# Summing MLP weight blocks in DRAM: fewer sums, and half of them moved into the MLP

## Chip, cores, metric

The kernel runs on one core of a Trainium2 chip. The metric is the device time of one execution in microseconds (us), as a median of runs.

## What is computed

One decoder layer over 2048 tokens of width 1024, in float32, followed by a final RMSNorm. Four token mixers share one input projection; the MLP has a squared ReLU between two weights of 1024x4096 and 4096x1024.

```python
h = rms_norm(x, norm1_g); z = h @ w_in
y = concat([sgu(z), s5(z), rglru(z), forgetting_attention(z)])
x = x + group_rms_norm(y, mix_norm_g) @ w_out
h = rms_norm(x, norm2_g)
x = x + square(relu(h @ w_mlp_in)) @ w_mlp_out
out = rms_norm(x, final_g)
```

## The kernel before

Every product is made of three matmuls on high and low parts (`wh`, `wl`, and the like), so each operand is read, cast on ScalarE (the high part) and subtracted on VectorE (the low part): the helper `split`, L53 to L58.

**Order of the stages.** Input projection with the small mixers and S5 (until about 600 us), attention with the output projection woven between its units, then the MLP. Up to the MLP the order on TensorE is written by hand, with a planner clock `ck` that counts planned TensorE time; other engines are ordered by the framework. Inside `MLP.run` the framework orders all engines, in its own plan of when data is ready, earlier-traced instructions first.

**The MLP.** Tokens are processed in two halves of 1024, and the hidden width in two chunks `c` of 2048. Each (half, chunk) has an "in" stage and an "out" stage. A stage is a 2x2 block product done by Strassen's scheme with 7 products `i` instead of 8: `FIRST` and `SECOND` say for each product which two blocks of the weight and of the other operand are added or subtracted, and to which results it goes. `IN_ORDER` and `OUT_ORDER` are the orders of the products. Each product has 8 steps `p` of 12 matmuls, so a stage has 56 steps and the MLP 448 (`steps`, index `n`). For the first half, steps 0 to 55 are the in stage of chunk 0, 56 to 111 its out stage, 112 to 167 the in stage of chunk 1.

**Weights of a step.** `make(n + 2)` requests the weight of a step two steps ahead. A weight that is one block is loaded with one DMA into the pool `rw` (5 buffers, 2 KB per partition) by `weight`. A weight that is a sum of two blocks is loaded with two DMAs into one tile of the pool `raw` (`m_raw`, 5 buffers, 4 KB per partition) by `weight_pair`, and added on GpSimd (`united`, L1492). `tokens_side` loads the other operand of the next product, 4 tiles for each product, through the same pool `raw`, added on GpSimd where it is a sum. The preparation of the second token half (`prep`) runs beside the first half's in stage, one piece at every second step from step 11 on: it holds four tiles `h` of the pool `raw` from their load until the last of eight groups of four transposes (`tp`), first for tokens 0 to 511 of the half, then for the others.

**Sums in DRAM.** To save the second load and the GpSimd addition, `weight_sums` builds some sums in DRAM tables: a copy of one block from the ScalarE queue (L1426, 512 KB, DRAM to DRAM) and, three jobs later, an accumulating DMA of the other block from the GpSimd queue (L1430). `S1` are four tables of the first weight for chunk 0 (products 2, 5, 6 and 7), `S2` eight tables of the second weight, four for each chunk. Each table takes 4 jobs: 16 for `S1`, 32 for `S2`. The planner clock calls one job every 9.0 planned us from 110 on; what is left when attention ends is issued there at once (L1794).

**Around the change.** In attention the queries and keys (`q`, `ks`) are loaded from a DRAM scratch `qk`, whose high parts `qh` are stored from the ScalarE queue and low parts `ql` from the GpSimd queue. `ngc` are cumulative gates, spread over the partitions. The output projection stores its result `x1` from the GpSimd queue (L1369, shown as x<-x), and SyncE loads it again (L1348, and as `h` for the MLP).

Of the kernel before, what the change touches and what calls it, by code (L numbers as in the profile page):

```python
# [5 lines left out]
F32 = mybir.dt.float32  # L6
# [36 lines left out]
def behind(tc, eng):  # L43

    ins = next(i for i in reversed(tc.nc.cur_bb.bb.instructions) if i.engine == eng)
    return tc.issue_after(ins)
# [1349 lines left out]
IN_ORDER = (1, 4, 5, 7, 3, 2, 6)  # L1396
# [1 line left out]
AHEAD = 2  # L1398


def weight_sums(tc, w1, w2, S1, S2):

    nc = tc.nc
    jobs = []
    for c in range(2):
        def second(x):
            return w2[(c * 2 + x[0]) * 1024:(c * 2 + x[0] + 1) * 1024, x[1] * 512:(x[1] + 1) * 512]

        def first(x):
            return w1[x[1] * 512:(x[1] + 1) * 512, (c * 2 + x[0]) * 1024:(c * 2 + x[0] + 1) * 1024]

        for S, side, table, n, at in ((S1, 0, FIRST, 128, first), (S2, 1, SECOND, 256, second)):
            for i in IN_ORDER:
                if (i, c) in S:
                    a, b, _ = table[i][side]
                    for r in range(4):
                        rs = slice(r * n, (r + 1) * n)
                        jobs.append((S[i, c][rs], at(a)[rs], at(b)[rs]))  # L1420
    LAG = 3
    for n in range(len(jobs) + LAG):
        if n < len(jobs):
            to, a, _ = jobs[n]
            with behind(tc, ACT):
                nc.scalar.dma_start(out=to, in_=a)  # L1426
        if n >= LAG:
            to, _, b = jobs[n - LAG]
            with behind(tc, POOL):
                nc.gpsimd.dma_start(out=to, in_=b, accum_op=ADD)  # L1430
        yield


class MLP:
# [1 line left out]

    def __init__(self, tc, cst, final_g, x1, hT, w1, w2, S1, S2, out, T=2048):
        self.tc, self.nc, self.cst, self.x1, self.hT, self.w1, self.w2, self.out, self.T = tc, tc.nc, cst, x1, hT, w1, w2, out, T  # L1440
        self.final_g, self.S1, self.S2 = final_g, S1, S2
        self.D, self.FF = w1.shape
        self.KD = self.D // 128
        self.HT = 1024
        self.NC = 2
        self.NP = self.FF // 128 // self.NC // 2
        self.es = ExitStack()
        self.P = lambda n, b, **k: self.es.enter_context(tc.tile_pool(name=n, bufs=b, reuse_waits="tile", **k))
        P = self.P
        self.bp = P("m_b", 2)  # L1450
        self.raw = P("m_raw", 5)
        self.rw = P("m_rw", 5)
        self.wp = P("m_w", 4)
        self.htp = P("m_ht", 2)
        self.sm = P("m_sm", 2)
        self.jkp = P("m_jk", 1)
        self.ps_i = P("m_psi", 3, space=PSUM)
        self.halves = list(reversed(range(T // self.HT)))
# [71 lines left out]
    def first_weight(self, c, i, p):  # L1530

        a, b, sign = FIRST[i][0]
        rows = lambda w, f: w[:, f:f + 128].rearrange("(k p) f -> p k f", p=128)
        if (i, c) in self.S1:
            return self.weight(rows(self.S1[i, c], p * 128))
        w = [rows(self.w1[x[1] * 512:(x[1] + 1) * 512], self.tile_row(c, p, x[0])) for x in (a, b) if x]
        return self.weight_pair(w, sign) if b else self.weight(w[0])

# [67 lines left out]
    def run(self):  # L1606
        nc, P, NP = self.nc, self.P, self.NP

        P("m_pad", 1).tile([128, 32], F32, tag="pad", name="pad")
        self.cp = P("m_c", 1)  # L1610
        self.sp = P("m_s", 3)
        self.shp = P("m_sh", 4)
        accp = P("m_acc", 1)
        gp = P("m_gf", 1)
        ps_o = P("m_pso", 5, space=PSUM)
        self.C, self.acc = {}, {}
        ends = {}
        for order, table, n in ((IN_ORDER, FIRST, 0), (OUT_ORDER, SECOND, 1)):
            seen, last = {}, {}
            for i in order:  # L1620
                for blk, _ in table[i][2]:
                    seen.setdefault(blk, i)
                    last[blk] = i
            ends[n] = {i: [b for b in seen if seen[b] == i] for i in order}, {i: [b for b in last if last[b] == i] for i in order}
        steps = [(half, c, out, i, p) for half in self.halves for c in range(self.NC) for out in range(2)
                 for i in (OUT_ORDER if out else IN_ORDER) for p in range(NP)]
        made, sides = {}, {}
        groups = [s[:4] for s in steps if s[4] == 0 and not s[2]]

        def side(n):  # L1630
            if n < len(groups):
                half, _, _, i = groups[n]
                g = self.tokens_side(half, i)
                sides[groups[n]] = next(g)
                return g
            return iter(())

        def make(n):
            if n >= len(steps):
                return  # L1640
            half, c, out, i, p = steps[n]
            if not out:
                made[n] = (self.first_weight(c, i, p),)
            else:
                made[n] = self.second_weight(c, i, p), self.hidden_side(i, p)

        gf = gp.tile([128, self.D], F32, tag="gf", name="gf")
        nc.sync.dma_start(out=gf, in_=self.final_g.partition_broadcast(128))
        for _ in side(0):
            pass  # L1650
        for n in range(AHEAD):
            make(n)
        nxt, more, part = 1, iter(()), iter(())
        for n, (half, c, out, i, p) in enumerate(steps):
            if c == 0 and not out and i == IN_ORDER[0] and p == 0:
                k = self.halves.index(half) + 1
                more = self.prep(self.halves[k]) if k < len(self.halves) else iter(())
            if c == 0 and not out and i == IN_ORDER[3]:
                self.acc[p] = accp.tile([128, self.D], F32, tag=f"acc{p}", name="acc")
                with behind(self.tc, SP):  # L1660
                    nc.sync.dma_start(out=self.acc[p], in_=self.x1[half * self.HT // 128 + p])
            if n % 2 and n > 10:
                next(more, None)
            make(n + AHEAD)
            if not out and p == 1:
                part = side(nxt)
                nxt += 1
            if not out and 1 <= p < 6:
                next(part, None)
            got = made.pop(n)  # L1670
            first, last = (e[i] for e in ends[out])
            if not out:
                self.product_in(i, p, got[0], sides[half, c, out, i], first, last)
                continue
            if p == 0:
                po = [ps_o.tile([128, 512], F32, tag="po", name="po") for _ in range(4)]
            self.product_out(p, *got, po)
            if p == NP - 1:
                for t in range(4):
                    for (rt, d), sign in SECOND[i][2]:  # L1680
                        self.gather(self.acc[4 * rt + t][:, d * 512:(d + 1) * 512], po[t], sign)
                    if c == self.NC - 1:
                        for rt in range(2):

                            if (rt, 0) in last and all((rt, 1) not in e for e in later(ends[1][1], i)) or \
                                    (rt, 1) in last and all((rt, 0) not in e for e in later(ends[1][1], i)):
                                self.finish(half, 4 * rt + t, gf)
        self.es.close()
# [10 lines left out]


RATES = 2.3, 0.5
SUMS = 110.0, 9.0
NX, NO, XB = 2, 3, 2


def hybrid_kernel(tc, A, out, T=2048):
    nc = tc.nc
    with ExitStack() as top:
# [9 lines left out]
                 v=dp.tile([T, 4, 2, 64], F32, name="v"), ys=dp.tile([T, 1024], F32, name="ys"),  # L1718
                 negc=dp.tile([4, T], F32, name="negc"), x1=[dp.tile([128, 1024], F32, name=f"x1_{t}") for t in range(T // 128)],
                 hT=[[dp.tile([128, 512], F32, name=f"hT_{k}_{q}") for q in range(T // 512)] for k in range(8)])  # L1720
        S1 = {(i, 0): dp.tile([512, 1024], F32, name=f"s1_{i}0") for i in IN_ORDER if FIRST[i][0][1] and i != 1}
        S2 = {(i, c): dp.tile([1024, 512], F32, name=f"s2_{i}{c}") for i in OUT_ORDER if SECOND[i][1][1] and i != 1 for c in range(2)}
        D5 = s5_scratch(dp)
        r8 = cp.tile([128, NPR], F32, name="r8")
# [11 lines left out]
            cst["ii"] = ii  # L1736

        ck = Clock()
        sums = weight_sums(tc, A["w_mlp_in"][0], A["w_mlp_out"][0], S1, S2)
        ck.set_slow(sums, *SUMS)  # L1740
        with tc.manual_schedule(engines={mybir.EngineType.PE}):
            side = ExitStack()
# [50 lines left out]
            ea.close()  # L1793
            for _ in sums:  # L1794
                pass
            M = MLP(tc, cst, A["final_g"], S["x1"], S["hT"], A["w_mlp_in"][0], A["w_mlp_out"][0], S1, S2, out, T)
            ps_t[0] = pool(eo, "o_pst", 2, space=PSUM, side="right")
            at.idle = False
            ps_o[0] = [(pool(eo, "o_pso2", NO, space=PSUM, side="right"), "po")]
# [40 lines left out]
```

## Time and profile before

| what | us |
| --- | --- |
| median of 3 runs | 2517.39 |
| lowest and highest of them | 2511.12, 2519.61 |
| profiled execution, its own time | 2509.57 |
| its span in the trace | 2507.9 |
| TensorE busy in the span | 2201.3 (88%) |

The span runs from the first to the last instruction of one profiled execution. Rows of stages give each engine's busy time in a stretch, the clock that TensorE was granted (1.00 is 2.4 GHz), the mean busy share of the 16 DMA engines and the rate that they moved. The in and out stages of the MLP were cut where the matmuls change from `pi` (in) to `po` (out).

### The profile page before, as it was taken

To read this page: it belongs to the slowest core of one execution; us is meant where nothing else is said; L and a number is where in the kernel's file an instruction comes from. 1 tells how busy PE (TensorE), PEld (TensorE's weight loads), DVE (VectorE), ACT (ScalarE), POOL (GpSimd) and SP (SyncE) were. 2 spreads that over 40 slices of the span, in tenths; PEclk is the share of its full clock that TensorE was granted. 3 is DMA by queue.
4 is the path that set the end of the run, shared out by engine and by line. 5 is a ranking of instruction groups with operands and counts; after the bars stand their busy time and mean duration, and the time that the engine had idled before them with its cause. 6 is when DMAs were issued, how large, how long until landed. Compare 5 with 4: busy or idle time off the path is not lost.

```text
span 2507.9 us, 32062 instructions
## 1 busy us (share of the span) xinstructions
PE 2201.3 (88%) x10077; PEld 1792.2 (71%) x10077; DVE 1672.5 (67%) x3776; ACT 1169.5 (47%) x2351; POOL 832.4 (33%) x908
## 2 busy tenths in 40 slices
PE   5798987894779978677899999999999999999997
PEld 5676766673567767565777778878778887888886
DVE  6686755662446655343668786787986769668697
ACT  4312534252345545332567434575355753457543
POOL 2143343232001101020312472554722237245462
PEclk8899998997789989798999999999999999999999
DMA  7535457546577776478876544874448533487323
GB/s 177 143 66 132 122 144 203 156 117 184 163 183 204 224 215 185 131 251 284 258 253 190 168 129 132 236 234 136 134 150 281 183 124 126 127 232 230 126 89 110
DMA packets 367963, 434.52 MB, mean 173 GB/s; under 512 B 42352, under 2 KB 244112, under 8 KB 367536
## 3 DMA queue, kind: packets, MB, share of 16 engines
q1 hardware_dynamic: 319696, 327.46, 42.9%
q0 software_dynamic: 32704, 73.54, 11.9%
q10 hardware_dynamic: 15392, 31.46, 4.0%
q8 instruction: 80, 1.31, 0.2%
q14 instruction: 91, 0.75, 0.1%
HBM read 369.30 MB, written 113.34 MB: 192 GB/s over the span
## 4 chain that ended last, share of the span: by engine, by line
PE 47%; DMA 15%; DVE 6%; issue 4%; POOL 3%; ACT 2%; SPq 1%; POOLq 0%; ACTq 0%; DVEq 0%
PE po L1591 6%; PE po L1592 6%; PE po L1593 6%; PE pi L1566 6%; PE pi L1567 6%; PE pi L1568 6%; DMA q<-qk 4%; DMA ngc<-negc 2%; DMA qk<-qh 2%; POOL raw L1492 2%; DMA x<-x 2%; PE t L50 1%; DMA y<-ys 1%; DMA raw<-hT 1%; PE s L1087 1%
## 5 line engine op out<-in xcount | busy, mean ns | idle before, releaser
L1492 POOL TENSOR_TENSOR raw<-raw 128x512 f32<-128x512 f32 x208 | 305.4, 1474 | 393.9 <-DMA raw<-hT 170.7
L58 DVE TENSOR_TENSOR wl<-raw,wh 128x512 fp32r<-128x512 f32 x448 | 386.2, 867 | 48.0 <-ACT wh L54 46.6
L1566 PE MATMUL pi<-bh,wh 128*128 128x512 f32 x896 | 353.4, 394 | 21.1 <-ACT wh L54 6.9
L1591 PE MATMUL po<-wh,sh 128*128 128x512 f32 x896 | 353.5, 395 | 19.9 <-DVE acc L1582 17.1
L1553 POOL TENSOR_TENSOR s<-c 128x512 f32<-128x512 f32 x160 | 255.3, 1599 | 316.2 <-DVE sl L58 272.8
L1568 PE MATMUL pi<-bh,wl 128*128 128x512 f32 x896 | 351.8, 393 | 1.2 <-DVE wl L58 1.2
L1592 PE MATMUL po<-wl,sh 128*128 128x512 f32 x896 | 351.6, 392 | 0.0
L1567 PE MATMUL pi<-bl,wh 128*128 128x512 f32 x896 | 351.4, 392 | 0.0
L1593 PE MATMUL po<-wh,sl 128*128 128x512 f32 x896 | 348.5, 392 | 0.0
L54 ACT CAST wh<-raw 128x512 fp32r<-128x512 f32 x448 | 275.9, 616 | 103.5 <-PE pi L1567 50.9
L58 DVE TENSOR_TENSOR sl<-s,sh 128x512 fp32r<-128x512 f32 x160 | 189.1, 1190 | 46.6 <-ACT sh L54 43.4
L54 ACT CAST sh<-s 128x512 fp32r<-128x512 f32 x160 | 99.4, 621 | 247.0 <-PE po L1592 219.6
L1566 PEld LDWEIGHTS pi<-bh,wh 128*128 128x128 f32 x896 | 169.8, 190 | 60.4 <-ACT c L1572 7.8
L1591 PEld LDWEIGHTS po<-wh,sh 128*128 128x128 f32 x896 | 169.9, 190 | 59.5 <-DVE acc L1582 19.9
L1568 PEld LDWEIGHTS pi<-bh,wl 128*128 128x128 f32 x896 | 169.6, 189 | 38.0 <-DVE wl L58 2.6
L1593 PEld LDWEIGHTS po<-wh,sl 128*128 128x128 f32 x896 | 169.7, 189 | 35.8
L1567 PEld LDWEIGHTS pi<-bl,wh 128*128 128x128 f32 x896 | 169.7, 189 | 35.4 <-DVE bl L58 0.3
L1592 PEld LDWEIGHTS po<-wl,sh 128*128 128x128 f32 x896 | 170.2, 190 | 34.7
L436 PE MATMUL z<-wh,hl 128*128 128x512 f32 (+1 forms) x384 | 154.0, 401 | 17.3 <-ACT hl L54 9.0
L1087 PE MATMUL s<-ks,q 128*128 128x512 f32 (+3 forms) x320 | 94.4, 410 | 79.0 <-DMA q<-qk 31.8
L1102 ACT ACTIVATE p<-p,ng 128x512 f32<-128x512 f32 (+3 forms) x160 | 103.7, 651 | 117.1 <-DVE ng L1098 117.1
L437 PE MATMUL z<-wl,hl 128*128 128x512 f32 (+1 forms) x384 | 144.8, 377 | 1.0 <-DVE wl L388 1.0
(359 smaller groups left out, 4356.8 us busy)
## 6 DMA issues: line engine op xcount, KB each, us to landing
raw<-in_w_mlp_in_dram SPq DMA_DIRECT2D x256, 256.0 KB
raw<-hT SPq DMA_DIRECT2D x192, 256.0 KB
raw<-s SPq DMA_DIRECT2D x192, 256.0 KB
raw<-in_w_mlp_out_dram SPq DMA_DIRECT2D x128, 256.0 KB
x<-in_x_dram SPq DMA_DIRECT2D x32, 512.0 KB
s<-in_w_mlp_out_dram ACTq DMA_DIRECT2D x32, 512.0 KB
s<-in_w_mlp_out_dram POOLq DMA_DIRECT2D x32, 512.0 KB, 11.4
x<-x POOLq DMA_DIRECT2D x31, 512.0 KB, 6.4
```

Of the source, the lines that this page charges most:

```text
L54: nc.scalar.copy(out=hi, in_=src)
L58: nc.vector.tensor_tensor(out=lo, in0=src, in1=hi.bitcast(F32), op=SUB)
L436: nc.tensor.matmul(pz, lhsT=hi[:, k, sl], rhs=wh, start=(k == 0), stop=False)
L437: nc.tensor.matmul(pz, lhsT=hi[:, k, sl], rhs=wl, start=False, stop=False)
L1492: self.nc.gpsimd.tensor_tensor(out=raw[:, 0], in0=raw[:, 0], in1=raw[:, 1], op=ADD if sign > 0 else SUB)
L1553: self.nc.gpsimd.tensor_tensor(out=s, in0=src, in1=self.C[b[1], b[0], p], op=ADD if sign > 0 else SUB)
L1566: nc.tensor.matmul(pt, lhsT=wh[:, sl], rhs=bh[:, k], start=(k == 0), stop=False)
L1567: nc.tensor.matmul(pt, lhsT=wh[:, sl], rhs=bl[:, k], start=False, stop=False)
L1568: nc.tensor.matmul(pt, lhsT=wl[:, sl], rhs=bh[:, k], start=False, stop=(k == 3))
L1591: nc.tensor.matmul(po[t], lhsT=sh[:, ts], rhs=vh, start=(p == 0), stop=False)
L1592: nc.tensor.matmul(po[t], lhsT=sh[:, ts], rhs=vl, start=False, stop=False)
L1593: nc.tensor.matmul(po[t], lhsT=sl[:, ts], rhs=vh, start=False, stop=(p == self.NP - 1))
```

## The change

The tables `S1` are dropped: the weights of products 2, 5, 6 and 7 of chunk 0 are again read as pairs and added on GpSimd, in both token halves. `weight_sums` makes the tables of the second weight only, for one chunk, on a queue given by the caller. It is called twice: for chunk 0 as before from the planner clock (every 10.0 planned us), and for chunk 1 inside `MLP.run`, where the copies go on the SyncE queue, one job at every third step from step 57 on.

```diff
-def weight_sums(tc, w1, w2, S1, S2):
+def weight_sums(tc, w2, S2, c, eng, queue):
...
-    for c in range(2):
...
-        for S, side, table, n, at in ((S1, 0, FIRST, 128, first), (S2, 1, SECOND, 256, second)):
-            for i in IN_ORDER:
-                if (i, c) in S:
...
+    for i in OUT_ORDER:
+        if (i, c) in S2:
+            a, b = (w2[(c * 2 + x[0]) * 1024:(c * 2 + x[0] + 1) * 1024, x[1] * 512:(x[1] + 1) * 512] for x in SECOND[i][1][:2])
+            for r in range(4):
+                rs = slice(r * 256, (r + 1) * 256)
+                jobs.append((S2[i, c][rs], a[rs], b[rs]))
     LAG = 3
     for n in range(len(jobs) + LAG):
         if n < len(jobs):
             to, a, _ = jobs[n]
-            with behind(tc, ACT):
-                nc.scalar.dma_start(out=to, in_=a)
+            with behind(tc, eng):
+                queue.dma_start(out=to, in_=a)
...
-        if (i, c) in self.S1:
-            return self.weight(rows(self.S1[i, c], p * 128))
         w = [rows(self.w1[x[1] * 512:(x[1] + 1) * 512], self.tile_row(c, p, x[0])) for x in (a, b) if x]
         return self.weight_pair(w, sign) if b else self.weight(w[0])
...
+        sums = weight_sums(self.tc, self.w2, self.S2, 1, SP, nc.sync)
...
+            if n > 7 * NP and n % 3 == 0:
+                next(sums, None)
             make(n + AHEAD)
...
-SUMS = 110.0, 9.0
+SUMS = 110.0, 10.0
...
-        sums = weight_sums(tc, A["w_mlp_in"][0], A["w_mlp_out"][0], S1, S2)
+        sums = weight_sums(tc, A["w_mlp_out"][0], S2, 0, ACT, nc.scalar)
         ck.set_slow(sums, *SUMS)
```

## Rows read from the trace of the kernel before

**Rows 1.** Busy time by stage: span, stretch, PE, PEld, DVE, ACT, POOL, clock, DMA.

```profile
540.00:660.00 120.00, 73.63 (x290) 57.00 (x288) 42.50 (x128) 35.12 (x90) 26.97 (x52) 0.77 0.58 162
660.00:1090.00 430.00, 350.11 (x1837) 291.32 (x1838) 234.51 (x749) 201.01 (x524) 48.22 (x105) 0.89 0.65 184
1090.00:1210.00 120.00, 82.91 (x360) 65.32 (x358) 40.13 (x93) 31.11 (x61) 25.98 (x34) 0.84 0.96 304
1210.00:1384.00 174.00, 164.88 (x712) 133.70 (x713) 122.64 (x184) 115.67 (x207) 41.20 (x29) 0.95 0.73 225
1384.00:1552.00 168.00, 159.87 (x700) 131.18 (x699) 135.46 (x159) 69.95 (x124) 84.19 (x54) 0.97 0.43 135
1552.00:1706.00 154.00, 152.91 (x673) 125.70 (x672) 114.66 (x154) 102.37 (x181) 86.60 (x60) 1.00 0.80 239
1866.00:2021.00 155.00, 150.58 (x662) 123.65 (x661) 114.56 (x206) 107.06 (x187) 44.53 (x35) 1.00 0.74 232
```

**Rows 2.** Issues of the DRAM sums: count, ns, first and last start.

```profile
L1426 ACTq DMA_DIRECT2D s<-in_w_mlp_out_dram x32: 497/498/8528, 433.6 to 1104.4; - x32
L1426 ACTq DMA_DIRECT2D s<-in_w_mlp_in_dram x16: 497/498/662, 78.5 to 418.4; - x16
...
L1430 POOL DMA_DIRECT2D s<-in_w_mlp_out_dram x32: 878/982/1992, 502.3 to 1123.2; - x32
```

**Rows 3.** DMA queues of the whole span: packets, MB, share of 16 engines.

```profile
q0 software_dynamic: 32704, 73.54, 11.9%
q10 hardware_dynamic: 15392, 31.46, 4.0%
```

**Rows 4.** Chain that ended last, 585 to 660 us: start, length, what.

```profile
589.24 18.29 DMA qk<-qh
...
608.24 28.27 DMA qk<-qh
```

**Rows 5.** Busy time in short stretches, columns as in rows 1.

```profile
612.00:626.00 14.00, 0.00 (x0) 0.00 (x0) 0.00 (x0) 0.00 (x0) 0.00 (x0) 0.50 0.27 94
...
1040.00:1060.00 20.00, 7.73 (x44) 6.50 (x44) 5.25 (x24) 6.06 (x16) 2.50 (x7) 0.79 0.54 149
...
1100.00:1120.00 20.00, 10.02 (x29) 7.83 (x30) 5.61 (x19) 3.37 (x7) 8.70 (x12) 0.74 1.05 381
```

**Rows 6.** Chain that ended last, 940 to 1064 us, first and last of five.

```profile
950.28 19.59 DMA q<-qk
...
1039.38 21.05 DMA q<-qk
```

**Rows 7.** Chain that ended last, 1085 to 1165 us.

```profile
1104.40 18.28 DMA s<-in_w_mlp_out_dram
...
1124.24 21.48 DMA x<-x
```

**Rows 8.** GpSimd's stores of x1 in the whole span: KB, median us to landing.

```profile
x<-x POOLq DMA_DIRECT2D x31, 512.0 KB, 6.4
```

**Rows 9.** SyncE's issues from 1226 to 1262 us, the four tiles of `prep`.

```profile
1227.32 3.33 SPq L1470 DMA_DIRECT2D h<-x  x3
...
1241.05 0.34 SPq L1470 DMA_DIRECT2D h<-x  x1
```

**Rows 10.** Instructions on the tile tp, 1210 to 1420 us: ns, first and last start.

```profile
L50 PE MATMUL tp<-ident,h x64: 270/272/273, 1276.0 to 1411.0; 128*128 128x128 f32 x64
```

**Rows 11.** TensorE in order of time: last transposes for the first four tiles.

```profile
1323.86 0.60 PE L50 MATMUL tp<-ident,h 128*128 128x128 f32 x4
```

**Rows 12.** Chain that ended last, 1255 to 1290 us: one load to the next.

```profile
1260.53 3.68 DMA raw<-hT
...
1267.44 3.06 DMA raw<-hT
```

**Rows 13.** GpSimd's additions (L1492) in two in stages: stretch, busy time, clock, DMA.

```profile
1210.00:1384.00 174.00, 36.89 (x26) 0.95 0.73 225
1552.00:1706.00 154.00, 82.03 (x57) 1.00 0.80 239
```

More of the change, by code (lines that the diff above doesn't have):

```diff
@@ L1398 @@
 AHEAD = 2
-def weight_sums(tc, w1, w2, S1, S2):
+def weight_sums(tc, w2, S2, c, eng, queue):
     nc = tc.nc
     jobs = []
-    for c in range(2):
[L1408 to L1412, printed above, removed]
-        for S, side, table, n, at in ((S1, 0, FIRST, 128, first), (S2, 1, SECOND, 256, second)):
-            for i in IN_ORDER:
-                if (i, c) in S:
[L1417 to L1420, printed above, removed]
+    for i in OUT_ORDER:
[4 more added lines that the diff above has]
+                jobs.append((S2[i, c][rs], a[rs], b[rs]))
     LAG = 3
@@ L1434, with __init__ @@
 class MLP:
-    def __init__(self, tc, cst, final_g, x1, hT, w1, w2, S1, S2, out, T=2048):
+    def __init__(self, tc, cst, final_g, x1, hT, w1, w2, S2, out, T=2048):
         self.tc, self.nc, self.cst, self.x1, self.hT, self.w1, self.w2, self.out, self.T = tc, tc.nc, cst, x1, hT, w1, w2, out, T
-        self.final_g, self.S1, self.S2 = final_g, S1, S2
+        self.final_g, self.S2 = final_g, S2
         self.D, self.FF = w1.shape
@@ L1720, in hybrid_kernel @@
                  hT=[[dp.tile([128, 512], F32, name=f"hT_{k}_{q}") for q in range(T // 512)] for k in range(8)])
-        S1 = {(i, 0): dp.tile([512, 1024], F32, name=f"s1_{i}0") for i in IN_ORDER if FIRST[i][0][1] and i != 1}
         S2 = {(i, c): dp.tile([1024, 512], F32, name=f"s2_{i}{c}") for i in OUT_ORDER if SECOND[i][1][1] and i != 1 for c in range(2)}
@@ L1795, in hybrid_kernel @@
                 pass
-            M = MLP(tc, cst, A["final_g"], S["x1"], S["hT"], A["w_mlp_in"][0], A["w_mlp_out"][0], S1, S2, out, T)
+            M = MLP(tc, cst, A["final_g"], S["x1"], S["hT"], A["w_mlp_in"][0], A["w_mlp_out"][0], S2, out, T)
             ps_t[0] = pool(eo, "o_pst", 2, space=PSUM, side="right")
```

## Prediction

> **What bounds the kernel now.** I read the busy time by stage first [rows 1]. From 1552 us on TensorE is busy nearly all the time at full clock (152.91 of 154 us in one in stage): there only work on TensorE counts, and nothing in the change touches that. Before, it stands idle: 46.4 of 120 us from 540 to 660, 79.9 of 430 in attention, 37.1 of 120 from 1090 to 1210, at a mean clock of 0.77 to 0.89. The first in stage of the MLP, 1210 to 1384, takes 174 us where the in stage with the same products but without `prep` takes 154. So the change can win before 1210 and can lose mainly in that one stage.
>
> The issues of the sums show where they lie [rows 2]: 16 copies for S1 from 78.5 to 418.4, one per 22.7 us, and 32 for S2 from 433.6 to 1104.4, one per 21.6 us. They run through attention and end in a burst behind it. The queue totals price them [rows 3]: the ScalarE queue moved 31.46 MB in 4.0% of 2507.9 us, 3.2 us per MB, the GpSimd queue 73.54 MB in 11.9%, 4.1 us per MB. A job is 0.52 MB on each: 1.7 + 2.1 = 3.8 us of all 16 engines.
>
> The chain then shows what TensorE waited for in those three stretches, and the SyncE issues, the transposes and the additions how much room the in stage has; they come with the terms.
>
> **Removed before the MLP.** 48 jobs become 16, called at 10.0 planned us instead of 9.0. The last copy is called at planned 260, the place of the old job 16.7, and the last accumulation at planned 290, the place of old job 20: at old times 433.6 + 4 x 21.6 = 520 us. So from about 540 us on no sum runs before the MLP. Until then the pace is that of before, and I count nothing.
>
> Term a, 540 to 660. The chain goes through two stores of `qk`, 18.29 and 28.27 us [rows 4], queued on ScalarE's queue between sum copies, and one such copy's issue took 8528 ns [rows 2], with ScalarE's casts behind it. In 46.6 us run two jobs, 7.6 us of the engines. Upper bound: those two jobs, the blocked issue, and a third of the stores' 46.6 us as queueing on top, 28. Lower bound 5: from 612 to 626 TensorE did nothing while the DMA engines were 0.27 busy [rows 5], so the store there is slow by itself, and only the start of the queue can move. That row is near, so I take 14, the two jobs and most of the blocked issue.
>
> Term b, attention. 430 / 21.6 = 20 jobs, 76 us of the engines, 0.18 of a share of 0.65 [rows 1]. If all waiting fell with the share (0.18 / 0.65 = 28%), of 80 us idle and up to 47 us lost to the lower clock, 35 us would come back. Lower bound 5: the `q` loads on the chain, five pieces between 19.59 and 21.05 at the ends [rows 6], last 20 us also where the DMA share is 0.54 [rows 5]. Between them I take 18.
>
> The Trainium skill ("DMA: Bandwidth & Descriptors", section "Why a DMA increments its semaphore by 16 and not by 1") says that a DMA is spread over the largest number of engines, at most 16, that divides the outer dimensions of both sides. The loads of `q` and the stores of `qk` have an outer dimension of 2 in DRAM, so two engines; the trace agrees as far as a 20 us load beside half-idle engines shows it. By that rule a and b would fall to their lower bounds, and the sum below would be +8.
>
> Term c, the burst. The last copies come at 1104.4, the accumulations end at 1123, and only then does GpSimd issue the store of `x1` that SyncE waits for: 18.28 + 21.48 us on the chain [rows 7], where a store usually lands in 6.4 us [rows 8]. That is 33 us less on this chain, but the stage has only 37 us of idle time, and at 1100 to 1120 the engines are over 1.00 busy also with loads that stay [rows 5]. After it `prep` and the last output projection set the pace. Upper bound 34, lower 8 (TensorE finds its next wait soon), and I take 20.
>
> **Added in the first in stage (term d).** Products 5, 7, 2 and 6 of chunk 0 load 8 pairs each through the pool `raw`: 32 more loads and 32 more GpSimd additions for each half. The additions alone cost nothing: chunk 1's in stage already has them, 82.03 us of them against 36.89 [rows 13], and its TensorE row is full. What that stage has not is `prep`. Its four tiles take four of the five `raw` buffers from 1241.05 [rows 9] to 1323.86 [rows 11]. In that time one load follows the other through a single buffer, 6.91 us from one to the next [rows 12]; now that is 4 tiles per product, 28 us against 8 steps of 2.75 us (154 / 56), and just holds. After the change it is 12 per product, 1.5 per step or 10.4 us. Over the 16 steps of products 5 and 7 that is 16 x (10.4 - 2.75) = 122 us, and the same for products 2 and 6 under the second four tiles: upper bound 244. The lower bound is nothing (a gain is excluded: no transfer goes away here).
>
> I take less because the transposes that end the hold wait for no weight. They stand at every second step (from 1276.0 on [rows 10], one group per 6 us); if TensorE starves, the framework's plan brings them forward. Say the hold halves to 41 us. Product 5 starts at 1210 + 16 x 2.75 = 1254, so 28 us of it fall on pairs: 4 loads, 2.7 steps, where 10.2 are due, 20 us late, less 5 us of transposes (8 groups of 0.60) done in the gap. 15 us, twice, and 3 us at half clock behind the gaps: 33. Bytes do not bind: 225 GB/s x 174 us and 8.4 MB more are 47.6 MB, 150 us at the 317 GB/s that 304 at a share of 0.96 makes.
>
> **Moved into the first out stage (term e).** 16 jobs, 61 us of the engines in 168: share 0.43 becomes 0.79, what chunk 1's in stage has (0.80) with a full TensorE [rows 1]. Behind a copy on SyncE's queue stand the weight loads of the next steps, whose five `rw` buffers cover 15 us; a copy as slow as 18.28 us [rows 7] would overhang by 3.3, 53 us for 16. GpSimd issues 16 x 1 us more [rows 2] beside 84 us of work; its accumulation waits for a copy made 9 steps, some 27 us, earlier. I take 3.
>
> **Second half (term f).** Its chunk 0 in stage now looks like chunk 1's, plus the loads of `acc`: 232 GB/s x 155 us + 8.4 MB is 44.4 MB, 140 of 155 us. 0 to 8, I take 2.
>
> **Sum.** -14 - 18 - 20 + 33 + 3 + 2 = -14 us. Against the profiled execution's own 2509.6 that is 2495.6; the median of the runs is 7.8 us above that execution, so 2503.
>
> **Rivals.**
> - *The single buffer holds (slower).* If the transposes stay near their written places, term d is nearer 122 than 33, for one group of tiles or shared by both: -14 + 89 = +75, about 2592, up to 2715 with both in full. For it: the row of 6.91 us, which leaves no room already. Against it: TensorE has nothing else to do then, so the plan should move them. It decides as soon as d is over 47 us.
> - *The pair loads hide (faster by more).* Loads are issued ahead of the hold, d is 3 and e and f nothing: -49, 2468. For it: the full TensorE of chunk 1. Against it: 10.4 us per step cannot be prefetched with five buffers.
> - *The slow loads are slow by themselves.* a and b 5 each: +8, 2525. For it rows 5 and 6; against it the blocked issue and 0.65 of share.
> - That the copies are not moved is excluded: a job at step 111 is the nineteenth and last call, before step 168 first reads a table of chunk 1.
>
> **Chances.** Forecast 0.42 (its own range 2480 to 2528), single buffer 0.20, hidden 0.18, slow by themselves 0.20. A measurement here tells 0.3%, 7.5 us, from no change. Faster: 0.27 of the first, 0.18, 0.03 of the last, 0.48. Same: 0.10 + 0.07 = 0.17. Slower: 0.35. The range reaches down to the hidden case and its larger gains, 2460, and up into the single-buffer case, 2570, with its upper half left out.
>
> **What would show it.** Copies and accumulations end by 540 us and return from about 1375 to 1540. The two `qk` stores on the chain are shorter by some 10 us, and the first in stage starts some 50 us earlier. That stage has about 58 additions on GpSimd, takes about 205 us, and TensorE waits in it for `wh` from paired loads, with `tp` closer together. An in stage under 185 us or over 240 us makes the forecast wrong, as does a start of the MLP less than 25 us earlier.

## The result, and the profile after

The changed kernel takes 2667.01 us (median of 4 runs, 2661.74 to 2669.33), the kernel before 2518.04 beside it (4 runs): a ratio of 1.0594, 95% interval 1.0568 to 1.062. It is slower by 149 us, where 14 us less was forecast. Its profiled execution has a span of 2663.4 us against 2507.9, 155.5 more.

Busy time by stage, at the borders of the kernel after (span, stretch, PE, PEld, DVE, ACT, POOL, clock, DMA, GB/s):

```profile
540.00:660.00 120.00, 79.80 (x343) 62.24 (x342) 50.16 (x156) 42.35 (x111) 24.28 (x52) 0.83 0.48 145
660.00:1090.00 430.00, 379.49 (x2018) 314.34 (x2016) 251.25 (x786) 215.77 (x552) 39.79 (x101) 0.94 0.56 178
1090.00:1123.00 33.00, 28.78 (x136) 23.17 (x136) 14.17 (x29) 8.82 (x16) 6.12 (x7) 0.91 0.86 304
1123.00:1523.00 400.00, 228.97 (x719) 168.91 (x720) 125.73 (x191) 123.58 (x215) 85.00 (x65) 0.73 0.41 126
1523.00:1698.00 175.00, 163.29 (x694) 132.31 (x693) 137.66 (x156) 67.11 (x117) 89.86 (x69) 0.95 0.81 218
1698.00:1852.00 154.00, 152.46 (x670) 125.34 (x670) 117.15 (x152) 101.26 (x178) 86.41 (x60) 1.00 0.79 236
```

The fourth row answers to the first in stage of [rows 1], and it holds the whole loss: 400 us where 174 stood. TensorE is idle for 171.0 us of it (before 9.1) and busy 64.1 us longer for nearly the same instructions, at a granted clock of 0.73 instead of 0.95. The DMA engines fall from 0.73 to 0.41, so no bytes bind. Everything ahead of that row got faster (clock 0.83 against 0.77, 0.94 against 0.89), and the rows behind it are nearly those of before.

What the engines waited for in that stage (us in total, times, longest):

```profile
POOL raw L1484 <- DMA raw<-in_w_mlp_in_dram: 219.7, 35, 29.1
...
PE pi L1556 <- ACT wh L54: 171.8, 32, 9.3
DVE wl L58 <- ACT wh L54: 127.7, 34, 6.8
ACT wh L54 <- POOL raw L1484: 118.4, 33, 6.1
```

The same wait of TensorE in the stage before:

```profile
PE pi L1566 <- ACT wh L54: 6.9, 1, 6.9
```

The first four rows are one chain: TensorE waits for `wh`, ScalarE's cast of it for GpSimd's addition, and GpSimd for the loads of pairs. The first of the 32 waits of TensorE, 7.05 us, is the start of the stage, as before. In the order of TensorE's matmuls the other 31 stand in front of 31 of the 32 steps whose pairs this half now loads (products 5, 7, 2 and 6), and in front of no other step. The chain that ended last shows why the pairs come late (start, length, what):

```profile
1205.84 3.37 DMA raw<-in_w_mlp_in_dram
...
1209.37 1.27 POOL raw L1484
...
1210.67 0.63 ACT wh L54
...
1211.32 0.70 DVE wl L58
...
1212.42 2.94 DMA raw<-hT
...
1215.49 1.29 POOL raw L1484
...
1216.80 0.63 ACT bh L54
...
1217.45 0.70 DVE bl L58
...
1218.60 3.27 DMA raw<-in_w_mlp_in_dram
```

A load takes about 3 us, no longer than before [rows 12]. But the next load starts only when VectorE has read the buffer of the last: in these rows one load per 6.4 us, one after the other. That is what a pool with a single free buffer looks like. Who holds the other four is seen in SyncE's issues of `prep`'s tiles, and when they come free in TensorE's transposes of them:

```profile
1145.41 3.37 SPq L1462 DMA_DIRECT2D h<-x  x3
...
1159.13 0.34 SPq L1462 DMA_DIRECT2D h<-x  x1
...
1352.69 1.95 SPq L1462 DMA_DIRECT2D h<-x  x4
```

```profile
1242.06 1.05 PE L50 MATMUL tp<-ident,h 128*128 128x128 f32 x4
...
1350.81 0.60 PE L50 MATMUL tp<-ident,h 128*128 128x128 f32 x4
```

```profile
L50 PE MATMUL tp<-ident,h x64: 270/272/421, 1242.1 to 1548.6; 128*128 128x128 f32 x64
```

Four of five buffers are held from 1159.13 to 1351, 192 us against 83 before [rows 9, 11]. The second four follow at once, from 1352.69 to 1549, 196 us against 87 [rows 10, 11]. Each hold is 109 us longer, 218 in all; the stage, from its first product to that of the next, grew by 219.5 (175 to 394.3). From 1340 to 1360 TensorE works mainly on product 3, whose weights are single blocks from the other pool. There it is busy for all 20.00 us at full clock, although the first four tiles are held until 1351: it is the steps with pairs that starve.

```profile
1340.00:1360.00 20.00, 20.00 (x94) 16.50 (x93) 13.24 (x22) 14.31 (x26) 1.29 (x1) 1.00 0.73 249
```

Before the MLP the change did what it says. The sums' issues (ns min/median/max, first and last start):

```profile
L1418 ACTq DMA_DIRECT2D s<-in_w_mlp_out_dram x16: 497/501/8524, 212.8 to 442.6; - x16
L1418 SPq DMA_DIRECT2D s<-in_w_mlp_out_dram x16: 496/497/1488, 1518.5 to 1658.2; - x16
...
L1422 POOL DMA_DIRECT2D s<-in_w_mlp_out_dram x32: 857/921/1725, 271.2 to 1675.5; - x32
```

The last copy ahead of the MLP is issued at 442.6, the last accumulation at 544.45; then no sum is issued until 1518.5. The MLP starts at 1127.8 instead of 1210.0. The score matmuls mark the attention's borders; in the trace of before they start from 626.5 to 1069.7, after:

```profile
L1087 PE MATMUL s<-ks,q x320: 220/395/796, 620.3 to 1012.2; 128*128 128x512 f32 x112, 128*128 128x128 f32 x16, 128*128 128x256 f32 x16, 128*128 128x384 f32 x16
```

So of the 82.2 us won, 6.2 lie ahead of attention, 51.3 in it (443.2 to 391.9) and 24.7 behind it (140.3 to 115.6). The queue totals fell too (packets, MB, share): GpSimd's queue is the first, ScalarE's the second, both below [rows 3].

```profile
q0 software_dynamic: 30400, 65.15, 9.6%
q10 hardware_dynamic: 8736, 14.68, 1.7%
```

### The profile page after: what moved, and what is told of

Same layout as the page of the kernel before. It is cut to its first block, busy times and chain, and to the rows that moved or that the text cites. A ratio compares the mean times of both kernels' runs of the same rounds, so it can differ in the third digit from the quotient of the medians.

```text
span 2663.4 us, 32203 instructions
## 1 busy us (share of the span) xinstructions
PE 2248.9 (84%) x10077; PEld 1809.3 (68%) x10077; DVE 1699.7 (64%) x3776; ACT 1171.6 (44%) x2351; POOL 895.8 (34%) x956
## 4 chain that ended last, share of the span: by engine, by line
PE 44%; DMA 15%; DVE 6%; issue 5%; POOL 5%; ACT 3%; SPq 2%; POOLq 0%; ACTq 0%; DVEq 0%
PE po L1581 6%; PE po L1582 6%; PE po L1583 6%; PE pi L1556 5%; PE pi L1558 5%; PE pi L1557 5%; DMA raw<-in_w_mlp_in_dram 5%; POOL raw L1484 3%; DMA q<-qk 3%; DVE wl L58 2%; DMA raw<-hT 2%; PE s L1087 2%; PE t L50 2%; PE po L1362 1%; PE po L1364 1%
## 5 line engine op out<-in xcount | busy, mean ns | idle before, releaser
L1484 POOL TENSOR_TENSOR raw<-raw 128x512 f32<-128x512 f32 x272 | 388.3, 1434 | 570.5 <-DMA raw<-in_w_mlp_in_dram 364.4
L1556 PE MATMUL pi<-bh,wh 128*128 128x512 f32 x896 | 378.0, 422 | 179.6 <-ACT wh L54 172.2
L58 DVE TENSOR_TENSOR wl<-raw,wh 128x512 fp32r<-128x512 f32 x448 | 403.7, 907 | 169.7 <-ACT wh L54 168.1
L1558 PE MATMUL pi<-bh,wl 128*128 128x512 f32 x896 | 372.9, 416 | 3.9 <-DVE wl L58 3.9
L1557 PE MATMUL pi<-bl,wh 128*128 128x512 f32 x896 | 370.7, 414 | 0.0
L1556 PEld LDWEIGHTS pi<-bh,wh 128*128 128x128 f32 x896 | 181.8, 203 | 235.4 <-ACT wh L54 187.9
L1557 PEld LDWEIGHTS pi<-bl,wh 128*128 128x128 f32 x896 | 182.2, 203 | 37.8
L436 PE MATMUL z<-wh,hl 128*128 128x512 f32 (+1 forms) x384 | 152.3, 397 | 16.7 <-ACT hl L54 8.5
L1572 DVE TENSOR_TENSOR c<-pi,c 128x512 f32<-128x512 f32 x128 | 87.5, 684 | 106.2 <-PE pi L1558 106.2
L58 DVE TENSOR_TENSOR bl<-raw,bh 128x512 fp32r<-128x512 f32 x112 | 101.9, 919 | 68.6 <-ACT bh L54 66.6
L438 PE MATMUL z<-wh,hl 128*128 128x512 f32 (+1 forms) x384 | 143.4, 373 | 1.6 <-DVE hl L58 1.6
```

Of the source, the lines that this page charges most:

```text
L58: nc.vector.tensor_tensor(out=lo, in0=src, in1=hi.bitcast(F32), op=SUB)
L436: nc.tensor.matmul(pz, lhsT=hi[:, k, sl], rhs=wh, start=(k == 0), stop=False)
L438: nc.tensor.matmul(pz, lhsT=lo[:, k, sl], rhs=wh, start=False, stop=(k == 7))
L1484: self.nc.gpsimd.tensor_tensor(out=raw[:, 0], in0=raw[:, 0], in1=raw[:, 1], op=ADD if sign > 0 else SUB)
L1556: nc.tensor.matmul(pt, lhsT=wh[:, sl], rhs=bh[:, k], start=(k == 0), stop=False)
L1557: nc.tensor.matmul(pt, lhsT=wh[:, sl], rhs=bl[:, k], start=False, stop=False)
```

## The experiments

Eight kernels, each beside runs of the kernel before on the same chip. "In stage" and "out stage" are the first of the MLP, from the first product of one to the first of the next. The theory is *hold*: `prep`'s four tiles leave one buffer to the pair loads. Its main rivals are that pairs and additions, or the sums that were moved into the MLP, are slow by themselves.

**1. The sums of the first weight alone taken out (e1_no_s1).** All else is the kernel before.

```diff
-        S1 = {(i, 0): dp.tile([512, 1024], F32, name=f"s1_{i}0") for i in IN_ORDER if FIRST[i][0][1] and i != 1}
+        S1 = {}
```

> The kernel before with the tables S1 dropped and nothing else: all 32 sums of the second weight still run ahead of the MLP. Single buffer (the four tiles of prep leave one of five raw buffers to the pair loads): the first in stage takes about 390 us, as after the change, against 175 before; the MLP starts some 35 us earlier because 16 jobs are gone, total about 2700. Moved sums to blame (chunk 1's sums inside the MLP cost the time): the in stage stays near 175, total about 2490.

Measured: 2697.26 us, ratio 1.0734 (1.0698 to 1.077). The in stage takes 394 us, as after, with the same waits:

```profile
1165.00:1559.00 394.00, 227.72 (x716) 169.26 (x717) 121.08 (x186) 121.11 (x211) 80.99 (x62) 0.73 0.40 123
```

```profile
PE pi L1566 <- ACT wh L54: 172.9, 32, 9.3
```

This one edit makes the whole loss of that stage; the sums inside the MLP have no part in it. The MLP starts at 1164.9, 45 us earlier than before (35 were expected).

**2. The other part alone (e2_moved_only).** The sums of the first weight stay; those of the second weight's chunk 1 move into the MLP.

```diff
-    for c in range(2):
+    for c in chunks:
...
-            with behind(tc, ACT):
-                nc.scalar.dma_start(out=to, in_=a)
+            with behind(tc, eng):
+                queue.dma_start(out=to, in_=a)
...
+        sums = weight_sums(self.tc, self.w1, self.w2, {}, {k: v for k, v in self.S2.items() if k[1] == 1}, (1,), SP, nc.sync)
...
+            if n > 7 * NP and n % 3 == 0:
+                next(sums, None)
```

> The kernel before with S1 kept, and only the sums of chunk 1 of the second weight moved into the first out stage on the SyncE queue. Single buffer: the first in stage stays at 175 us, the first out stage grows by some 8 us as after the change (167 to 175), the MLP starts 40 us earlier, total about 2490. Moved sums to blame: total above 2600.

Measured: 2464.88 us, ratio 0.9802 (0.9779 to 0.9826). The in stage takes 176.5 us, the out stage with the 16 moved sums 173 (before 167). So moving the sums costs some 7 us there and wins 48.5 ahead of the MLP (it starts at 1161.5; 40 were expected).

**3. `prep` moved behind the in stage (e3_prep_later).** The changed kernel, with its pairs and additions, but no hold in that stage.

```diff
-            if n % 2 and n > 10:
+            if n % 2 and n > 7 * NP:
```

> The kernel after the change, with prep of the second token half begun at step 57 (first out stage) and not at step 11: the same loads, additions and sums, at another time. Single buffer: the first in stage falls from 394 to about 158 us, like the other three in stages, the out stage pays 10 us for the transposes, total about 2440, faster than both kernels. If pair loads and GpSimd additions are too slow by themselves (512-byte rows, 1.3 us additions), the in stage stays near 390 and the total near 2660.

Measured: 2450.85 us, ratio 0.9751 (0.973 to 0.9773). It beats both kernels. The in stage takes 159.6 us with the same 32 pairs; its row, the wait that was 171.8 us, and the transposes, now all behind it:

```profile
1132.00:1292.00 160.00, 157.08 (x673) 127.03 (x674) 120.97 (x151) 104.94 (x186) 91.81 (x62) 0.98 0.92 273
```

```profile
PE pi L1556 <- ACT wh L54: 8.4, 2, 8.0
```

```profile
L50 PE MATMUL tp<-ident,h x64: 270/272/421, 1327.3 to 1482.1; 128*128 128x128 f32 x64
```

Pairs and additions by themselves are free here: GpSimd's 91.81 us of work and a DMA share of 0.92 fit into the 160 us, where the starved stage spread 85.00 us and 0.41 over 400. The out stage, which now has both `prep` and the sums, takes 193 us, 18 more than after (10 were expected).

**4. One more buffer (e4_raw6).** The changed kernel with six `raw` buffers, and three `rw` to make room: two are free under the hold.

```diff
-        self.raw = P("m_raw", 5)
-        self.rw = P("m_rw", 5)
+        self.raw = P("m_raw", 6)
+        self.rw = P("m_rw", 3)
```

> The kernel after the change with six raw buffers in place of five (and rw cut from five to three to make room, which touches single-block weights only). Single buffer: two buffers are left under prep, so a load every 3.4 us and not 6.9; 1.5 loads per step make 5.1 us per step and not 10.4 over the 32 steps concerned, the first in stage about 240 us, total about 2520. Pair loads too slow by themselves: unchanged, 390 us and 2660.

Measured: 2523.92 us, ratio 1.0049 (1.0032 to 1.0066). The in stage takes 245 us (about 240 were expected).

```profile
1125.00:1370.00 245.00, 190.80 (x705) 143.28 (x706) 126.22 (x184) 119.44 (x209) 85.98 (x64) 0.88 0.65 199
```

A second buffer takes back 149 of the 219.5 us, the dose that *hold* asks for.

**5. A shorter hold (e5_prep_each).** A piece of `prep` at every step instead of every second.

```diff
-            if n % 2 and n > 10:
+            if n > 10:
```

> The kernel after the change with a piece of prep at every step from 11 on, not at every second: each group of four tiles is held for some 14 steps and not 28. Single buffer: of the 32 steps with pair loads only some 15 (product 5 and most of 7) fall under a hold, so of 235 us lost 15 x 7.65 = 115 are left: first in stage about 270 us, total about 2545. Were the amount of work beside it the cause and not the hold, the stage would stay near 394.

Measured: 2549.18 us, ratio 1.015 (1.0105 to 1.0194); in stage 286 us (about 270 were expected). The tiles are issued from 1150.3 to 1269.9, and the last transposes start at 1360.8:

```profile
1133.00:1419.00 286.00, 197.29 (x737) 149.37 (x737) 128.59 (x185) 121.94 (x214) 91.64 (x65) 0.81 0.59 182
```

Half the steps under the hold leave half the loss: 111 of 219.5 us.

**6. What the sums cost attention (e6_copies_only).** The kernel before, without the accumulating transfers of the second weight's 32 sums.

```diff
-        if n >= LAG:
+        if n >= LAG and n - LAG < 16:
```

> The kernel before with the accumulating DMAs of all 32 sums of the second weight left out (their tables then hold one block only; the copies stay on the ScalarE queue). From the first to the last score matmul: 443 us before, 392 after the change. If the sums cost attention by engine time (1.7 us of a copy, 2.1 of an accumulation), about 415. If it is GpSimd's queue, about 392 to 400. If it is the copies on ScalarE's queue, about 443. From the last score matmul to the first matmul of the MLP: 140 before, 116 after; near 116 if the burst's accumulations held the x1 stores.

Measured, one run: 2455.4 us.

```profile
L1087 PE MATMUL s<-ks,q x320: 220/395/797, 612.6 to 1030.7; 128*128 128x512 f32 x112, 128*128 128x128 f32 x16, 128*128 128x256 f32 x16, 128*128 128x384 f32 x16
```

Attention takes 418.1 us: 25 of the 51 come back, near the 415 that engine time would make. The way from there to the MLP is 120 us, so 20 of the 24.7 come back.

**7. One plain copy instead of the pair (e7_plain_gpsimd).** For the same 32 sums GpSimd's queue copies, nothing accumulates, and ScalarE's queue copies nothing.

```diff
-        if n < len(jobs):
+        if n < min(len(jobs), 16):
...
-                nc.gpsimd.dma_start(out=to, in_=b, accum_op=ADD)
+                if n - LAG < 16:
+                    nc.gpsimd.dma_start(out=to, in_=b, accum_op=ADD)
+                else:
+                    nc.gpsimd.dma_start(out=to, in_=b)
```

> The kernel before with one plain copy from the GpSimd queue for each of the 32 sums of the second weight, in the accumulation's place, and no copy on the ScalarE queue (the tables hold one block only). First to last score matmul: about 415 by engine time; 420 to 443 if it is GpSimd's queue; about 392 if it is the ScalarE queue.

Measured, one run: 2449.9 us.

```profile
L1087 PE MATMUL s<-ks,q x320: 221/395/796, 616.5 to 1018.6; 128*128 128x512 f32 x112, 128*128 128x128 f32 x16, 128*128 128x256 f32 x16, 128*128 128x384 f32 x16
```

Attention takes 402.1 us, 41 of the 51 back, and fits none of the three expectations. Against none (391.9), ScalarE's copies alone cost 26 us, plain copies on GpSimd's queue 10, both parts of a sum together 51. Neither part alone explains the cost. Each of these is one profile, but the five kernels without a sum in attention (after, 3, 4, 5 and 8) took 391.4 to 392.9 us there, so these differences are well over that spread. The way to the MLP is 127.6 us: here only 13 of the 24.7 come back.

**8. The sums spread thinner (e8_later_every4).** Experiment 3 with a sum at every fourth step.

```diff
-            if n > 7 * NP and n % 3 == 0:
+            if n > 7 * NP and n % 4 == 0:
```

> The version with prep from step 57 on, with the sums of chunk 1 at every fourth step instead of every third, so that they end in the next in stage. If the 192 us of its first out stage (175 without prep beside the sums, 167 without both) come from sums and prep sharing the DMA engines, that stage falls to about 185 and the total by 5 us to 2446; if from the transposes and casts of prep, nothing changes, 2451.

Measured: 2465.46 us, ratio 0.9818 (0.9784 to 0.9852), worse than experiment 3 by 14.6 us, which neither expectation gives. The out stage falls only from 193 to 188 us, and the next in stage, into which the sums now reach, grows from 157 to 173. In experiment 5 `prep` is over before the first out stage, and that stage, with all 16 sums, takes 165 us: the sums alone do not lengthen it. How much of the 193 is `prep`'s own work beside them, no run separates.

## Why the prediction was wrong

**Term d, the step that failed.** The prediction worked out the hold (four of five buffers, one load per 6.91 us, 122 us for each group of tiles, 244 at most) and then cut it to 33, because "if TensorE starves, the framework's plan brings them forward", and "Say the hold halves to 41 us". That step failed. The term measured 219.5 us, 0.9 of the upper bound. The transposes were not brought forward: in the order of TensorE's instructions the first four tiles' groups stand between product steps 23 and 37, the second four's from 50 on, and in the kernel before they stand at nearly the same steps (23 to 37, 51 on). They were not late for want of work to do: VectorE had the first four tiles ready at 1173.6, and TensorE was idle for 32 of the 68 us from there to the first transpose at 1242.06.

```profile
L1469 DVE TENSOR_SCALAR h<-h,rs x4: 746/748/754, 1169.7 to 1172.9; 128x1024 f32<-128x1024 f32 x4
```

```profile
1173.70:1242.00 68.30, 35.99 (x89) 24.76 (x89) 12.72 (x19) 11.03 (x19) 13.87 (x11) 0.68 0.27 82
```

So the hold ends only when product 5's and 7's pairs have come through the one buffer that the hold leaves, and it lengthens itself from 83 to 192 us. Experiment 1 shows that the removed sums of the first weight alone do it, experiment 3 that without the hold the pairs cost nothing, experiments 4 and 5 that the loss follows the number of free buffers and the steps under the hold. Why the plan leaves the transposes where they are stays open; no run changed the plan itself. One candidate stands in the kernel and was not tried: `tp` takes its buffers from the pool of three that the products' `pi` use.

The arithmetic in front of that step held. Products 5, 7, 2 and 6 start at 1177.59, 1256.96, 1359.45 and 1443.02 and took 79, 79, 84 and 79 us, 10.0 us a step, where the prediction had 10.4 (1.5 loads of 6.91 us). One reading in it was off: "28 us against 8 steps of 2.75 us", which are 22, does not just hold. The stage with `prep` already took 20 us longer before the change than the one without, 9 of them idle.

The term's parts can be read from the two rows of the stage, whose windows differ by 226 us: 162 us are idle time, and 64 us are longer busy time, most of it the lower clock in the work between the gaps (0.73 against 0.95). The prediction gave the clock 3 us.

The rival "the single buffer holds" named the mechanism, the place and the row. Its written time of 2592 was one hold's worth, its "up to 2715 with both in full" the nearer one: the measured 2667 lies 75 us above the one and 48 below the other.

**Terms a to c, the gain ahead of the MLP.** They measured 6.2, 51.3 and 24.7 us, 82 instead of 52. The terms named for a's upper bound add up to 32 (7.6 + 8.5 + 15.5), not 28; a is near its lower bound of 5: the two `qk<-qh` stores of [rows 4] are gone from the chain, but in their place stand a store of `qk<-ql` of 10.02 us, a wait of 11.76 in SyncE's queue and a load of `ks` of 17.56. How much of the 6.2 is the sums' is not settled: attention starts at 626.5 to 634.5 us in the three kernels whose sums run until then (before, experiments 1 and 2), at 620.3 to 627.9 in the five without, and at 612.6 and 616.5 in experiments 6 and 7, which have parts of the sums there. c lies between its bounds, 5 over the value taken; the other kernels without sums behind attention need 113 to 117 us there too.

b was mis-sized, at 51 against 18 and above its upper bound of 35. That bound scaled the idle time with the share of bytes, and the real price of a sum is larger: 18 copies and 18 accumulations start in that stretch (20 jobs were counted), 2.8 us for each pair. The price goes with the number: with 7 copies and 10 accumulations left there, experiments 1 and 2 take 417.5 and 414.6 us, half-way between 391.9 and 443.2. On the chain of attention the loads of `q` fall from 22.2% of 444 us to 18.1% of 392, 99 to 71 us (five loads of 19.7 us on average, then four of 17.8), and those of `ngc` from 10.9% to 7.8%, 48 to 31. So most of the gain lies in the time of these two loads on the chain, which the DMA share of 0.65 did not show.

By the Trainium skill ("DMA: Bandwidth & Descriptors", section "Why a DMA increments its semaphore by 16 and not by 1"), a load with an outer dimension of 2 has two engines. The trace after agrees as far as a load's length can show it: with no sum running, `q` loads on the chain still take 17.77 us, and 53.31 for three, where loads of pairs in the MLP, two of the same 256 KB, land in about 3. No row counts a load's engines. What the prediction drew from that rule, that b would then be 5, did not come true: b was 51.3.

**Terms e and f.** The out stage took 8.7 us more (166.6 to 175.3) where 3 was said, the second half's first in stage 4.5 (157.7 to 162.2) where 2 was said. The other five stages grew by 5 in all. The sum: -82.2 + 219.5 + 8.7 + 4.5 + 5 = 155.5, as measured. The 8.7 are not the sums' alone: in experiment 5, with the same sums and `prep` over, that stage takes 165 us.

**The other rivals.** "The pair loads hide" and "the slow loads are slow by themselves" both fall, the first by the 219.5 us, the second by b's 51.3 us where it had 5.

**The signs it gave itself.** The sums ended by 545 us as said, and came back from 1518 to 1676 (said: 1375 to 1540). The MLP began 82 us earlier (said: 50). GpSimd's additions there rose to 61, 80.67 us, about as forecast. `tp` did not come closer together (the first eight groups stretch over 109 us, 48 before), and the stage, at 394 us, was far over the 240 that it named as wrong.

## What to carry to other kernels

Before loads are added to a shared pool, count the buffers that its longest-lived tile holds, and multiply the loads that fall under the hold by the time of one pass through what is left; a hold that waits for steps which themselves wait for the pool grows with the starvation it causes. Do not discount that product by what a scheduler might reorder without a trace that shows it reorder. Where the price is too high, move the long-lived tile, not the loads: here one changed condition turned a ratio of 1.0594 into 0.9751.

## What the runs showed of the hardware that was not expected

Transfers whose result attention does not use cost that stage 51 us, 12% of it, while the DMA engines there were busy for a share of 0.65 with them and 0.52 without. Half of the price came back without the accumulating transfers (share 0.56 of 419 us), four fifths when a plain copy on GpSimd's queue stood in for the pair (0.58 of 403 us). Both kept the engines busy for 234 us and cost 26 and 10 us, so it was not their busy time alone. What else it was, no run shows.

In the starved stage TensorE was granted 0.73, and nearly the same instructions took 64 us more of its time (228.97 against 164.88); with a free second buffer the clock was 0.88 and they took 190.80 us, with the hold gone 0.98 and 157.08 (that stage without the transposes).
